# Hybrid S5 / mLSTM encoder layer: gates on 64 rows, the input factor folded into the pole powers, Toeplitz blocks copied from SBUF to SBUF, and a new planned order

## The chip, the cores and the metric

One core of one Trainium2 chip runs the whole layer in one launch. The metric is device microseconds (us) for one execution. Engines are named as the profile names them: PE (TensorE matmul, PEld its weight loads), DVE (VectorE), ACT (ScalarE), POOL (GpSimd) and SP (SyncE), whose queue issues every DMA of this kernel.

## What is computed

The reference, cut to what matters here (x is 1024 x 1024 float32; h = rmsnorm(x)):

```python
proj = h @ w_in                       # 1024 x (512 S5 | 512 x_m | 512 o | 16 gates)
# S5 group: 32 groups of 16 channels, 64 complex poles each, two directions
f = (exp(lam dt) - 1) / lam           # the input factor
s = scan(exp(lam dt), f * (B u))      # forward and reverse
y = Re(C s_f) + Re(C s_b) + d u ; y = gelu(y) ; y = y * sigmoid(y @ w_glu + b_glu)
# mLSTM group: 4 heads, two directions, chunks of 128 steps
lf = log_sigmoid(f_pre) ; b = cumsum(lf within a chunk)
m_t = max(b + m_state, max over s <= t of (b_t - b_s + li_s))   # the running maximum
m_new = max(b_last + m_state, ...) ; weights exp(d - m_t), exp(a - m_t), exp(g - m_new)
x = x + rmsnorm(concat(y_s5, y_ml) @ w_out)
x = x + rmsnorm((silu(h @ w_gate) * (h @ w_up)) @ w_down)
```

## The kernel before, in words

The kernel is recorded first and issued afterwards. Class `K` calls an engine's operation, `Rec.add` records it with a due time (`Rec.at`, from the table `PLAN`, L48), and `Rec.schedule` (L284) places all operations one after another with a cost for each (`Rec.cost`, L229; `Rec.transfer`, L267, for a DMA) under limits on SBUF pages and PSUM banks. Out comes one fixed order for each engine; `Rec.emit` (L424) issues it, so nearly every row of the profile has the line L454. Each engine works through its order strictly: a waiting instruction holds all that stands behind it, DMA issues on SP included.

The stages, in order of time:

- `w_in_a` and `w_in_tile` (L581, L660): the input projection in three products of split fp32r operands, with x and the weights loaded beside it. `evac` (L631) scales the result; the gate columns go to two 64-row tiles of which 4 rows in 32 are live.
- `s5_prelude` (L779): poles, powers 0 to 8 of each pole (`GG`), input factor `F1`, `F2`, and two tables `C1`, `C2` of 128 x 1024, which are C times the input factor (L933 to L939); a table of cosines and sines goes to DRAM (`csd`).
- `gates` (L688): log-sigmoid, cumulative sums, running maxima, four kinds of exponentials, on tiles of 64 rows by 1024 steps, eight live rows; then 16 transposes on PE and 16 small copies on ACT into `col`, and rows written to DRAM (`rowd`, `decd`) for the heads.
- `s5_main` (L980): 16 blocks. Block b makes `o1` from `G1 C1 + G2 C2`, multiplies it by B on PE, and evacuates a 16 x 2 x 240 tile `sp`. From `sp` a Toeplitz block `T` of 128 x 128 for each of two groups is made by a DMA to DRAM (`std`, L1024) and two DMAs back with overlapping rows (L1028). `T` is the weight of the first of the six output matmuls (L1055).
- `mlstm_head` (L1063): four heads, interleaved with the blocks of `s5_main`; then `glu_out`, `out_proj`, `ffn_up` and `ffn_down` (seven passes).

```python
nc.sync.dma_start(out=std[g0:g0 + 2].rearrange("g c n -> c g n"), in_=sp)          # L1024
T = self.t([128, 2, 128])
for g in range(2):
    a = std[g0 + g, :, 0:128]
    nc.sync.dma_start(out=T[:, g], in_=view(a, 0, [[16, 8], [1, 128]]))            # L1028
nc.tensor.matmul(o, lhsT=T[:, g], rhs=u[:, g], start=True, stop=False)             # L1055
```

Of the kernel before, what the change touches and what calls it, by code (L numbers as in the profile page):

```python
# [16 lines left out]
L = 1024  # L17
# [16 lines left out]
CV = dict(gpre=0, hnorm=8, skip=12, convw=16, convb=36, bglu=40, gfpre=44, gbias=52)  # L34
NCV = 53
# [124 lines left out]
class Rec:  # L160
# [68 lines left out]
    def cost(self, o):  # L229
# [3 lines left out]
        if o.fn == "dma_start":  # L233
            o.dur = 0.05
# [31 lines left out]
    @staticmethod  # L266
    def transfer(src, dst):  # L267

        def run(ap):
            r = 1  # L270
            for s, c in reversed([list(x) for x in ap]):
                if c > 1 and s != r:
                    break
                r *= c
            return r
        outer = [next((c for s, c in ap if c > 1), 1) for ap in (src, dst)]
        k = max(i for i in range(1, 17) if not outer[0] % i and not outer[1] % i)
        n = 1
        for s, c in dst:
            n *= c  # L280
        r = min(run(src), run(list(dst)[1:]) if len(list(dst)) > 1 else run(dst), 1024)
        return k, n / r / k * (0.008 + 4 * r * 0.0369e-3)

    def schedule(self):  # L284
# [32 lines left out]
        while len(order) < len(self.ops):  # L317
# [139 lines left out]
class K:  # L457
# [73 lines left out]
    def body(self):  # L531
# [22 lines left out]
        self.decd = self.d([2, 4, 8])  # L554
# [76 lines left out]
    def evac(self, kind, i, P):  # L631
# [7 lines left out]
        elif kind == "g":  # L639
            self.gi, self.gf = self.t([64, L]), self.t([64, L])  # L640
# [47 lines left out]
    def gates(self):  # L688
        nc, cv = self.nc, self.cv
        gi, gf = self.gi, self.gf  # L690
        self.col = self.t([128, 8, 2, 4, 4])
        self.dcol = self.t([128, 2, 4, 8])
        bi = cv[0:64, CV["gbias"]:CV["gbias"] + 1]
        bf = self.t([64, 1])
        nc.vector.tensor_copy(out=bf, in_=cv[64:128, CV["gbias"]:CV["gbias"] + 1])
        QA, QB = self.t([128, L]), self.t([128, L])
        a = QA[0:64]
        nc.vector.tensor_scalar(gf, gf, bf, None, ALU.add)
        nc.scalar.activation(a, gf, AF.Abs)
        nc.scalar.activation(a, a, AF.Exp, scale=-1.0)  # L700
        nc.scalar.activation(a, a, AF.Ln, bias=1.0)
        nc.vector.scalar_tensor_tensor(gf, gf, 0.0, a, ALU.min, ALU.subtract)
        mask = QB[0:64]
        nc.gpsimd.memset(mask, 1.0)
        nc.gpsimd.memset(mask[0:32].rearrange("p (c t) -> p c t", t=128)[:, :, 0:1], 0.0)
        nc.gpsimd.memset(mask[32:64].rearrange("p (c t) -> p c t", t=128)[:, :, 127:128], 0.0)
        b = gf
        f, r = slice(0, 32), slice(32, 64)
        nc.vector.tensor_tensor_scan(b[f], mask[f], gf[f], 0.0, ALU.mult, ALU.add)
        nc.vector.tensor_tensor_scan(b[r, ::-1], mask[r, ::-1], gf[r, ::-1], 0.0, ALU.mult, ALU.add)  # L710
        ev = QA[0:64]
        nc.vector.scalar_tensor_tensor(ev, gi, bi, b, ALU.add, ALU.subtract)
        z = mask
        nc.gpsimd.memset(z, 0.0)
        c3 = lambda ap: ap.rearrange("p (c t) -> p c t", t=128)
        nc.vector.tensor_copy(out=c3(z[f])[:, 1:8, 0:1], in_=c3(b[f])[:, 0:7, 127:128])
        nc.vector.tensor_copy(out=c3(z[r])[:, 0:7, 127:128], in_=c3(b[r])[:, 1:8, 0:1])
        M = gi
        nc.vector.tensor_tensor_scan(M[f], z[f], ev[f], 0.0, ALU.add, ALU.max)
        nc.vector.tensor_tensor_scan(M[r, ::-1], z[r, ::-1], ev[r, ::-1], 0.0, ALU.add, ALU.max)  # L720
        mp = self.t([64, 8, 1])
        ml = self.t([64, 8, 1])
        dc = self.t([64, 8, 1])
        nc.vector.memset(mp, 0.0)
        nc.vector.tensor_tensor(mp[f, 1:8], c3(M[f])[:, 0:7, 127:128], c3(b[f])[:, 0:7, 127:128], ALU.add)
        nc.vector.tensor_tensor(mp[r, 0:7], c3(M[r])[:, 1:8, 0:1], c3(b[r])[:, 1:8, 0:1], ALU.add)
        nc.vector.tensor_copy(out=ml[f], in_=c3(M[f])[:, :, 127:128])
        nc.vector.tensor_copy(out=ml[r], in_=c3(M[r])[:, :, 0:1])
        nc.vector.tensor_tensor(dc, mp, ml, ALU.subtract)
        nc.scalar.activation(dc, dc, AF.Exp)  # L730
        nc.vector.tensor_tensor(c3(QA[64:128]), mp.to_broadcast([64, 8, 128]), c3(M), ALU.subtract)
        nc.scalar.activation(QA[64:128], QA[64:128], AF.Exp)
        nc.vector.tensor_tensor(c3(QB[0:64]), c3(ev), ml.to_broadcast([64, 8, 128]), ALU.subtract)
        nc.scalar.activation(QB[0:64], QB[0:64], AF.Exp)
        nc.vector.tensor_tensor(QB[64:128], b, M, ALU.add)
        nc.scalar.activation(QB[64:128], QB[64:128], AF.Exp, scale=-1.0)
        for d in range(2):
            nc.sync.dma_start(out=self.rowd[0, d], in_=M[32 * d:32 * d + 4])
            nc.sync.dma_start(out=self.rowd[1, d], in_=QA[64 + 32 * d:64 + 32 * d + 4])
            nc.sync.dma_start(out=self.decd[d], in_=dc[32 * d:32 * d + 4].rearrange("p c o -> p (c o)"))  # L740
        nc.sync.dma_start(out=self.dcol.rearrange("p d h c -> p (d h c)"), in_=self.decd.rearrange("d h c -> (d h c)").partition_broadcast(128))
        for qi, Q in enumerate((QA, QB)):
            for c4 in range(2):
                P = self.psum()
                for c in range(4):
                    cc = 4 * c4 + c
                    nc.tensor.transpose(P[:, c * 128:(c + 1) * 128], Q[:, cc * 128:(cc + 1) * 128], self.ident)
                for c in range(4):
                    cc = 4 * c4 + c
                    src = P[:, c * 128:(c + 1) * 128].rearrange("p (q d x) -> p q d x", q=2, d=2)[:, :, :, 0:4]  # L750
                    nc.scalar.copy(out=self.col[:, cc, :, :, 2 * qi:2 * qi + 2].rearrange("p d h q -> p q d h"), in_=src)
# [27 lines left out]
    def s5_prelude(self):  # L779
# [60 lines left out]
        GG = [(self.t([64, 8, 2, 64]), self.t([64, 2, 64])) for _ in range(2)]  # L840
        for (g, g8), t in zip(GG, (CS, SN)):
            V.tensor_tensor(g[:, :, 0], MG[:, 0:8], t[:, 0:8], ALU.mult)
            V.tensor_tensor(g8, MG[:, 8:9].to_broadcast([64, 2, 64]), t[:, 8:9].to_broadcast([64, 2, 64]), ALU.mult)
        GR = self.t([64, 8, 2, 64])
        for r in range(2):
            nc.scalar.copy(out=GR[:, :, r], in_=GG[r][0][:, :, 0])
        for x in (0, 1):
            nc.sync.dma_start(out=self.Gd[:, :, x, :], in_=GR[x::4].rearrange("p j r s -> p j (r s)"))
        GB = self.t([64, 8, 2, 64])
        for r in range(2):  # L850
            nc.scalar.copy(out=GB[:, :, r], in_=GG[r][0][:, 7::-1, 0])
        for x in (2, 3):
            nc.sync.dma_start(out=self.Gd[:, :, x, :], in_=GB[x::4].rearrange("p j r s -> p j (r s)"))
        for g, g8 in GG:
            nc.scalar.copy(out=g[:, :, 1], in_=g[:, :, 0])
# [22 lines left out]
        F1 = self.t([64, 2, 64])  # L878
        F2 = self.t([64, 2, 64])
# [3 lines left out]
        V.tensor_tensor(F1[:, 0], a, den, ALU.mult)  # L883
# [661 lines left out]
```

## Time and profile before

| what | value |
|---|---|
| median of three runs | 1159.42 us (1158.59 to 1164.47) |
| profiled execution: its own time | 1158.98 us |
| profiled execution: span of its instructions | 1157.2 us |
| busy, share of the span | PE 94%, PEld 75%, DVE 78%, ACT 48%, POOL 1% |
| granted TensorE clock, mean | 0.971 |

The profiled execution's own time is 1.8 us more than its span, and 0.4 us under the median. Busy shares are means over stages with different limits: the table of windows in the section of rows cuts the span by stage, and the chain of waits tells what ended last in one. An instruction's duration overlaps the next one's start by some hundredths of a us, so that a sum of durations is a little more than the time taken.

### The profile page before, as it was taken

Reading aid. Unit: us, or ns where it says so; the run is one execution under the profiler, and the core shown is the slowest. Engines: PE = TensorE matmul, PEld = TensorE weight load, DVE = VectorE, ACT = ScalarE, POOL = GpSimd, SP = SyncE. Lnnn points to the kernel's source line nnn. Section 1 sums busy time; section 2 is a strip of 40 time slices with the busy share of each in tenths; the row PEclk is TensorE's granted clock in tenths of the full one; section 3 lists DMA queues with packets and bytes.
Section 4 is the critical chain, followed back from the end, with each engine's and each line's share of the span. In section 5 each row is a group of like instructions: output and inputs, shape, how many; then the busy total and the mean of one; then the engine's idle time right before and its main releaser. Section 6 shows DMA issues by size and latency. Waiting matters only on the chain.

```text
span 1157.2 us, 14999 instructions
## 1 busy us (share of the span) xinstructions
PE 1082.9 (94%) x5037; PEld 872.1 (75%) x5037; DVE 897.1 (78%) x1943; ACT 554.6 (48%) x1158; POOL 13.0 (1%) x29
## 2 busy tenths in 40 slices
PE   8988798966879999988999999999999999999997
PEld 6767686755768778767888888778787888888885
DVE  7999789889999876877857575666666589866764
ACT  6637343755759765584223232323232249443631
POOL 0000000010000000000000000000000000000000
PEclk9989899978889999999999999999999999999999
DMA  8317845774137213344332323323241488566633
GB/s 328 132 56 237 221 126 134 196 194 124 39 93 303 73 55 121 132 146 183 119 121 98 109 83 108 111 82 110 82 137 56 168 313 309 171 214 203 214 118 145
DMA packets 102109, 172.59 MB, mean 149 GB/s; under 512 B 10417, under 2 KB 39665, under 8 KB 102033
## 3 DMA queue, kind: packets, MB, share of 16 engines
q1 hardware_dynamic: 102032, 171.65, 45.2%
q8 instruction: 39, 0.64, 0.2%
q14 instruction: 38, 0.30, 0.1%
HBM read 129.63 MB, written 41.98 MB: 148 GB/s over the span
## 4 chain that ended last, share of the span: by engine, by line
PE 60%; DVE 17%; DMA 11%; ACT 7%; issue 2%; SPq 2%; DVEq 0%; ACTq 0%
PE P L454 60%; DVE s L454 17%; ACT s L454 7%; DMA s<-d 3%; DMA d<-s 3%; SPq L454 2%; DMA s<-in_w_gate 2%; DMA s<-in_xT 2%; DMA s<-in_wB 1%; DMA s<-in_B 1%; ACT L454 0%; DMA s<-in_w_up 0%; DVEq L1541 0%; ACTq L454 0%; DVEq L454 0%
## 5 line engine op out<-in xcount | busy, mean ns | idle before, releaser
L454 PE MATMUL P<-s,s 128*128 128x512 f32 (+4 forms) x4862 | 1066.5, 376 | 60.9 <-DVE s L454 27.4
L454 PEld LDWEIGHTS P<-s,s 128*128 128x128 f32 (+1 forms) x4862 | 839.3, 188 | 264.0 <-DVE s L454 35.0
L454 DVE TENSOR_TENSOR s<-s,s 128x512 fp32r<-128x512 f32 (+9 forms) x879 | 543.1, 660 | 131.4 <-ACT s L454 120.9
L454 ACT CAST s<-s 128x512 fp32r<-128x512 f32 (+4 forms) x439 | 237.6, 582 | 199.2 <-DVE s L454 71.1
L454 DVE TENSOR_TENSOR s<-P,s 128x512 f32<-128x512 f32 (+2 forms) x210 | 128.3, 622 | 84.1 <-PE P L454 55.2
L454 ACT ACTIVATE s<-s 128x1024 f32<-128x1024 f32 (+7 forms) x134 | 91.2, 689 | 186.4 <-DVE s L454 185.4
L454 ACT COPY s<-P 128x512 f32<-128x512 f32 (+6 forms) x143 | 58.9, 447 | 148.8 <-PE P L454 143.4
L454 DVE TENSOR_TENSOR s<-s 128x8 f32<-128x8 f32 (+6 forms) x194 | 66.2, 349 | 12.3 <-DMA s<-in_w_down 6.6
L454 PE MATMUL P<-s 128*128 128x512 f32 (+2 forms) x175 | 63.8, 394 | 6.2 <-DVE s L454 6.2
L454 ACT ACTIVATE s<-s,s 128x128 f32<-128x128 f32 (+3 forms) x118 | 57.3, 551 | 21.8 <-DVE s L454 9.9
L454 ACT ACTIVATE s<-P,s 128x128 f32<-128x128 f32 (+1 forms) x168 | 51.3, 390 | 9.8 <-PE P L454 8.7
L454 ACT ACTIVATE s<-P 128x512 f32<-128x512 f32 (+2 forms) x70 | 39.6, 570 | 29.8 <-PE P L454 29.2
L454 DVE SCALAR_TENSOR_TENSOR s<-s,s,s 128x1024 f32<-128x1024 f32 (+4 forms) x42 | 42.9, 1047 | 1.1 <-ACT s L454 0.9
L454 PEld LDWEIGHTS P<-s 128*128 128x128 f32 (+1 forms) x175 | 33.1, 206 | 13.4 <-DVE s L454 6.6
L454 DVE TENSOR_TENSOR_SCAN s<-s,s 128x128 f32<-128x128 f32 (+1 forms) x68 | 33.5, 518 | 0.0
L454 DVE TENSOR_SCALAR s<-s 128x1 f32<-128x1 f32 (+13 forms) x140 | 24.4, 189 | 9.8 <-ACT s L454 8.9
L454 DVE SCALAR_TENSOR_TENSOR s<-P,s,s 128x128 f32<-128x128 f32 (+1 forms) x56 | 26.7, 515 | 3.6 <-PE P L454 2.6
L454 DVE SCALAR_TENSOR_TENSOR s<-s,s 128x1024 fp32r<-128x1024 f32 (+5 forms) x30 | 23.0, 786 | 0.0
L454 ACT ACT_TABLE_LOAD x14 | 18.0, 1283 | 1.0 <-PEq L1535 0.8
L454 DVE TENSOR_TENSOR s<-s,P 128x512 f32<-128x512 f32 (+2 forms) x43 | 15.9, 377 | 1.3 <-PE P L454 1.2
L454 ACT COPY s<-s 64x512 f32<-64x512 f32 (+1 forms) x24 | 13.7, 589 | 0.3
L454 POOL TENSOR_SCALAR_AFFINE_SELECT s<-s 128x1024 f32<-128x1024 f32 (+1 forms) x9 | 10.0, 1109 | 272.0 <-DMA s<-in_wqkv 159.2
(19 smaller groups left out, 74.2 us busy)
## 6 DMA issues: line engine op xcount, KB each, us to landing
s<-d SPq DMA_DIRECT2D x125, 256.0 KB
d<-s SPq DMA_DIRECT2D x77, 256.0 KB
s<-in_w_down SPq DMA_DIRECT2D x77, 256.0 KB
s<-d SPq DMA_DIRECT2D x36, 512.0 KB
d<-s SPq DMA_DIRECT2D x28, 512.0 KB
s<-in_w_gate SPq DMA_DIRECT2D x44, 256.0 KB
s<-in_w_up SPq DMA_DIRECT2D x44, 256.0 KB
s<-in_x SPq DMA_DIRECT2D x16, 512.0 KB
```

The costliest lines, as they stand in the source:

```text
L454: getattr(getattr(nc, o.eng), o.fn)(*[g(x) for x in o.a], **{n: g(x) for n, x in o.k.items()})
```

## The change

Four edits, and a new table for the planner. `ffn_up`, `ffn_down` and `out_proj` are not edited.

1. **Gates on 64 rows.** The 16 gate rows are evacuated by two instructions into a 16 x 1024 tile and written to DRAM (`gated`); they come back as two tiles of 64 rows (direction, head, chunk) by 128 steps. Sums and maxima are taken within a row. The carry from chunk to chunk goes to DRAM (`carryd`), back as 4 rows of 8 chunks for each direction, through a scan of 7 elements, to DRAM and back as one value a row. Two transposes and one copy fill `col`.
2. **Input factor in the pole powers.** The factor multiplies the powers (64 x 9 x 64, before the transposes) instead of C. `C1` and `C2` are now loaded as they are, 128 x 1024 each, twice the bytes of `CA` and `CB` before.
3. **Toeplitz blocks SBUF to SBUF.** `std` is gone; the two DMAs of a block read `sp` itself.
4. **The planner.** An issue of a DMA costs SP 0.6 in its model (0.05 before, with a queue of 0.5 behind it); bytes are dearer; the due times and limits in `PLAN` are others.

```diff
-    win=37.832, near=7.61, res=4, tie=0.042, tensor=0.771, vector=0.602, scalar=0.107, gpsimd=0.264, sync=3.052,
-    old=14.133, pre=0.431, pre_s=0.206, gate=19.374, w=35.224, w_r=10.241, wo=109.077, wo_r=14.436, conv=75.464,
+    win=37.832, near=6.997, res=3, tie=0.042, tensor=0.771, vector=0.707, scalar=0.119, gpsimd=0.425, sync=4.338,
+    old=14.133, pre=0.234, pre_s=0.216, gate=47.675, w=35.224, w_r=9.539, wo=90.593, wo_r=19.245, conv=49.493,
...
-            o.dur = 0.05
+            o.dur = 0.6
-        return k, n / r / k * (0.008 + 4 * r * 0.0369e-3)
+        return k, n / r / k * (0.008 + 4 * r * 0.042e-3)
...
-                nc.vector.tensor_tensor(self.gi[:, c], P[hf][0:64], R[0:64, c], ALU.mult)
-                nc.vector.tensor_tensor(self.gf[:, c], P[hf][64:128], R[64:128, c], ALU.mult)
+                nc.vector.tensor_tensor(gt[:, c], P[hf][0:16], R[0:16, c], ALU.mult)
+        if kind == "g":
+            nc.sync.dma_start(out=self.gated, in_=gt)
...
     def gates(self):
-        nc.vector.tensor_scalar(gf, gf, bf, None, ALU.add)
-        nc.scalar.activation(a, gf, AF.Abs)
-        nc.vector.tensor_tensor_scan(b[f], mask[f], gf[f], 0.0, ALU.mult, ALU.add)
-        nc.vector.tensor_tensor_scan(M[f], z[f], ev[f], 0.0, ALU.add, ALU.max)
-        nc.vector.tensor_tensor(c3(QA[64:128]), mp.to_broadcast([64, 8, 128]), c3(M), ALU.subtract)
-        for qi, Q in enumerate((QA, QB)):
-            for c4 in range(2):
-                    nc.tensor.transpose(P[:, c * 128:(c + 1) * 128], Q[:, cc * 128:(cc + 1) * 128], self.ident)
+        gi, gf = self.load(rows(self.gated[0:8]), [64, 128]), self.load(rows(self.gated[8:16]), [64, 128])
+        V.tensor_tensor_scan(b[f], one[f], gf[f], 0.0, ALU.mult, ALU.add)
+        V.tensor_tensor_scan(S[f], one[f], ev[f], -3.0e38, ALU.mult, ALU.max)
+        nc.sync.dma_start(out=self.carryd[0], in_=two)
+            nc.sync.dma_start(out=X[32 * d:32 * d + 4], in_=self.carryd[0, 32 * d:32 * d + 32].rearrange("(h c) x -> h c x", c=8))
+        V.tensor_tensor_scan(mp8[0:4, 1:8], X[0:4, 0:7, 0], X[0:4, 0:7, 1], 0.0, ALU.add, ALU.max)
+            nc.sync.dma_start(out=self.carryd[1, 32 * d:32 * d + 32, 0].rearrange("(h c) -> h c", c=8), in_=mp8[32 * d:32 * d + 4])
+        nc.sync.dma_start(out=mp, in_=self.carryd[1, :, 0:1])
+        V.tensor_scalar(M, S, mp, None, ALU.max)
+        nc.tensor.transpose(P[:, 0:64], ev, self.ident[0:64, 0:64])
+        nc.tensor.transpose(P[:, 64:192], Q, self.ident)
...
+        for i, (p, q, op) in enumerate(((fr, fi, ALU.add), (fi, fr, ALU.subtract))):
+            V.tensor_tensor(F, GG[0], bc9(p), ALU.mult)
+            V.tensor_tensor(T, GG[1], bc9(q), ALU.mult)
+            V.tensor_tensor(H1[0][:, :, i], F[:, 0:8], T[:, 0:8], op)
+            V.tensor_tensor(H1[1][:, i], F[:, 8], T[:, 8], op)
...
-        for d in range(2):
-            V.tensor_tensor(c1[:, :, d], ca, f1b, ALU.mult)
-            V.tensor_tensor(tt, cb, f2b, ALU.mult)
-            V.tensor_tensor(c1[:, :, d], c1[:, :, d], tt, ALU.add)
-            V.tensor_tensor(c2[:, :, d], ca, f2b, ALU.mult)
-            V.tensor_tensor(tt, cb, f1b, ALU.mult)
-            V.tensor_tensor(c2[:, :, d], c2[:, :, d], tt, ALU.subtract)
+        nc.sync.dma_start(out=self.C1, in_=I["CA"])
+        nc.sync.dma_start(out=self.C2, in_=I["CB"])
...
-            nc.sync.dma_start(out=std[g0:g0 + 2].rearrange("g c n -> c g n"), in_=sp)
             T = self.t([128, 2, 128])
             for g in range(2):
-                a = std[g0 + g, :, 0:128]
-                nc.sync.dma_start(out=T[:, g], in_=view(a, 0, [[16, 8], [1, 128]]))
+                nc.sync.dma_start(out=T[:, g], in_=view(sp[:, g, 0:128], 0, [[16, 8], [1, 128]]))
```

**Where the order moves.** On DVE, the middle of `gates` before (s_1_145 and s_2_600 are the two gate tiles, s_1_91 the mask, P_70 and P_63 the PSUM of `evac`):

```order
L454 SCALAR_TENSOR_TENSOR s_2_600<-s_2_600,s_1_364 64x1024
L454 TENSOR_TENSOR s_1_118<-P_70,s_1_286 128x64x8
L454 SCALAR_TENSOR_TENSOR s_2_600<-s_1_91,s_2_600 32x1024 x2
L454 TENSOR_TENSOR s_1_118<-P_63,s_1_286 128x64x8
L454 SCALAR_TENSOR_TENSOR s_1_364<-s_1_145,s_1_83,s_2_600 64x1024
L454 COPY s_1_91<-s_2_600 32x7 x2
```

and now (s_1_84 holds the small tiles; s_2_678 and s_1_325 are angles of `s5_prelude`):

```order
L453 SCALAR_TENSOR_TENSOR s_2_521<-s_1_84 64x128
L453 COPY s_1_84<-s_1_84 32x1
L453 TENSOR_SCALAR s_1_118<-s_2_678 128x8x32
L453 SCALAR_TENSOR_TENSOR s_2_521<-s_1_84,s_2_521 32x128 x2
L453 TENSOR_TENSOR s_1_84<-s_1_84,s_2_521 32x1
L453 TENSOR_TENSOR s_2_678<-s_2_678,s_1_118 128x8x32
L453 TENSOR_TENSOR s_1_84<-s_1_84,s_2_521 32x1
```

The scans are an eighth as long and stand among the angles of `s5_prelude`; 20 more DVE instructions of that kind stand between the last of these rows and the scan of 7 elements that needs the carry back from DRAM.

On SP, the writes of `gates` before (d_76 is `rowd`, d_77 `decd`, d_75 `ud`, in_wB the weights of `w_in_tile`):

```order
L454 DMA d_75<-s_1_118 128x1024
L454 DMA d_76<-s_1_145 4x1024 x2
L454 DMA d_77<-s_1_83 4x8 x2
L454 DMA d_76<-s_1_364 4x1024 x2
L454 DMA d_75<-s_1_120 128x1024
L454 DMA s_1_83<-d_77 128x64
L454 DMA s_1_218<-in_wB 128x512
```

and the carry of `gates` now (d_79 is `carryd`, d_81 `csd`):

```order
L453 DMA d_79<-s_1_84 64x2
L453 DMA d_81<-s_1_90 128x4x256
L453 DMA s_1_84<-d_79 4x16 x2
L453 DMA d_81<-s_1_251 128x4x256
L453 DMA d_81<-s_1_325 128x4x256
L453 DMA d_75<-s_3_684 128x1024
L453 DMA s_1_118<-in_wB 128x512 x2
L453 DMA d_79<-s_1_84 32x1x1 x2
L453 DMA s_1_233<-d_81 64x2x512 x2
```

The carry's write, its two loads and its second write now stand in one queue with the cosine tables that the first S5 blocks load; the weights of tile 3 of the input projection, which stood right behind the gates before, are ahead of them now.

On SP, a Toeplitz block before (d_80 is `std`):

```order
L454 DMA d_80<-s_2_1183 16x2x240
L454 DMA s_1_118<-d_75 128x2x128
L454 DMA s_1_118<-d_80 128x1x128 x2
L454 DMA d_80<-s_2_1146 16x2x240
L454 DMA d_74<-s_2_1183 8x16x128 x2
L454 DMA s_2_393<-d_80 128x1x128 x2
```

and now (d_74 is `yd`, d_80 now the pole powers `Gd`):

```order
L453 DMA s_1_90<-s_1_173 128x1x128 x2
L453 DMA s_3_1063<-in_wB 128x512
L453 DMA s_1_90<-d_75 128x2x128
L453 DMA s_3_749<-in_wB 128x512
L453 DMA s_1_243<-d_80 128x1x512
L453 DMA s_1_148<-in_B 128x1x384
L453 DMA s_1_233<-s_3_749 128x1x128 x2
```

The write is gone, and with it SP's wait for its landing.

## Rows read from the trace of the kernel before

**Rows 1.** Table of windows: us, PE, PEld, DVE, ACT, POOL busy, clock, DMA share, GB/s.

```profile
44.00:345.00 301.00, 251.09 (x1349) 202.82 (x1348) 280.27 (x645) 158.90 (x344) 8.65 (x13) 0.91 0.50 136
345.00:400.00 55.00, 53.64 (x321) 45.53 (x321) 51.19 (x187) 46.45 (x102) 2.18 (x2) 0.99 0.58 210
400.00:527.00 127.00, 119.55 (x541) 94.43 (x539) 97.44 (x268) 84.37 (x243) 0.00 (x0) 1.00 0.35 118
527.00:1150.00 623.00, 621.10 (x2663) 500.13 (x2662) 428.24 (x710) 230.55 (x408) 0.00 (x0) 1.00 0.42 147
```

**Rows 2.** Chain of waits in 44 to 345 us: shares of that stretch.

```profile
by line: DVE s L454 36.7%; PE P L454 26.3%; DMA s<-d 8.6%; DMA d<-s 7.1%; ACT s L454 6.2%; SPq L454 6.0%; issue 4.6%; DMA s<-in_wB 2.2%; DMA s<-in_B 2.2%; ACT L454 0.4%; DVEq L454 0.0%; ACTq L454 0.0%
```

**Rows 3.** Chain of waits at three Toeplitz blocks: start us, us, what.

```profile
120.54 9.69 DMA s<-d
...
130.94 5.59 DMA d<-s
...
136.59 2.14 DMA s<-d
...
232.83 3.82 DMA d<-s
236.66 2.11 DMA s<-d
...
245.45 7.81 DMA d<-s
253.33 1.92 DMA s<-d
```

**Rows 4.** Waits in 44 to 345 us: total us, times, longest.

```profile
PE P L454 <- DMA s<-d: 17.1, 6, 6.1
```

**Rows 5.** Timeline: start us, us, engine, instruction, count [idle before <- releaser].

```profile
81.75 4.96 PE L454 MATMUL P<-s,s 128*128 128x128 f32 x19 [3.63 <-ACT s L454]
90.46 2.07 PE L454 MATMUL P<-s,s 128*128 128x512 f32 x4 [3.76 <-ACT s L454]
138.86 1.30 PE L454 MATMUL P<-s,s 128*128 128x128 f32 x4 [5.81 <-DMA s<-d]
140.80 0.18 DVE L454 TENSOR_TENSOR s<-P,s 16x32 f32<-16x32 f32 x1 [2.96 <-ACT s L454]
225.38 0.18 DVE L454 TENSOR_TENSOR s<-P,s 16x32 f32<-16x32 f32 x1 [3.35 <-ACT s L454]
242.13 0.18 DVE L454 TENSOR_TENSOR s<-P,s 16x32 f32<-16x32 f32 x1 [1.63 <-ACT s L454]
259.72 0.18 DVE L454 TENSOR_TENSOR s<-P,s 16x32 f32<-16x32 f32 x1 [1.55 <-ACT s L454]
```

**Rows 6.** Groups by form, DVE, 40 to 100 us: count | busy us, mean ns | idle before.

```profile
L454 DVE TENSOR_TENSOR s<-s,s 128x512 f32<-128x512 f32 x20 | 12.9, 680 | 0.0
...
L454 DVE TENSOR_TENSOR_SCAN s<-s,s 32x1024 f32<-32x1024 f32 x4 | 9.1, 2272 | 0.0
...
L454 DVE TENSOR_TENSOR s<-s,s 64x1024 f32<-64x1024 f32 x3 | 3.7, 1219 | 0.1
L454 DVE TENSOR_TENSOR s<-P,s 64x512 f32<-64x512 f32 x4 | 2.7, 686 | 0.1
...
L454 DVE SCALAR_TENSOR_TENSOR s<-s,s,s 64x1024 f32<-64x1024 f32 x1 | 1.2, 1250 | 0.0
...
L454 DVE TENSOR_SCALAR s<-s,s 64x1024 f32<-64x1024 f32 x1 | 0.7, 709 | 0.0
```

**Rows 7.** Groups by form, DVE, whole span: forms nearest to the new instructions.

```profile
L454 DVE TENSOR_TENSOR_SCAN s<-s,s 128x128 f32<-128x128 f32 x64 | 24.4, 408 | 0.0
...
L454 DVE TENSOR_TENSOR s<-s,s 64x576 f32<-64x576 f32 x4 | 3.0, 741 | 0.0
...
L454 DVE TENSOR_SCALAR s<-s 64x128 f32<-64x128 f32 x4 | 0.9, 216 | 0.0
...
L454 DVE TENSOR_TENSOR s<-s,s 64x128 f32<-64x128 f32 x3 | 0.8, 280 | 0.6 <-ACT s L454 0.5
```

More of the change, by code (lines that the diff above doesn't have):

```diff
@@ L553, in body @@
         self.rowd = self.d([2, 2, 4, L])
-        self.decd = self.d([2, 4, 8])
+        self.decd = self.d([64, 1])
+        self.gated = self.d([16, L])
+        self.carryd = self.d([2, 64, 2])
         self.xm, self.xc, self.to, self.yml = [None] * 4, [None] * 4, [None] * 4, [None] * 4
@@ L710, in gates @@
[L710 to L718, printed above, removed]
@@ L742, in gates @@
-        for qi, Q in enumerate((QA, QB)):
-            for c4 in range(2):
-                P = self.psum()
-                for c in range(4):
-                    cc = 4 * c4 + c
-                    nc.tensor.transpose(P[:, c * 128:(c + 1) * 128], Q[:, cc * 128:(cc + 1) * 128], self.ident)
[L748 to L751, printed above, removed]
+        V, A = nc.vector, nc.scalar
@@ new lines, in gates @@
+        A.activation(a, a, AF.Exp, scale=-1.0)
+        A.activation(a, a, AF.Ln, bias=1.0)
+        V.tensor_scalar(gf, gf, bf, 0.0, ALU.add, ALU.min)
+        V.tensor_tensor(gf, gf, a, ALU.subtract)
+        one = self.ones
+        V.tensor_tensor_scan(b[f], one[f], gf[f], 0.0, ALU.mult, ALU.add)
+        V.tensor_tensor_scan(b[r, ::-1], one[r], gf[r, ::-1], 0.0, ALU.mult, ALU.add)
+        V.scalar_tensor_tensor(ev, gi, bi, b, ALU.add, ALU.subtract)
+        V.tensor_tensor_scan(S[f], one[f], ev[f], -3.0e38, ALU.mult, ALU.max)
@@ new lines, in gates @@
+        V.tensor_scalar(M, S, mp, None, ALU.max)
+        for h, e in ((f, 127), (r, 0)):
+            V.tensor_scalar(ml[h], M[h, e:e + 1], -1.0, None, ALU.mult)
+        A.activation(dc, mp, AF.Exp, bias=ml)
+        A.activation(wi, M, AF.Exp, scale=-1.0, bias=mp)
+        A.activation(Q[0:64], ev, AF.Exp, bias=ml)
+        V.tensor_tensor(b, b, M, ALU.add)
+        A.activation(Q[64:128], b, AF.Exp, scale=-1.0)
+        rowd = [self.rowd[i].rearrange("d h (c t) -> (d h c) t", t=128) for i in range(2)]
@@ L839, in s5_prelude @@
         V.tensor_tensor(MG[:, 5:8], MG[:, 1:4], MG[:, 4:5].to_broadcast([64, 3, 64]), ALU.mult)
[L840 to L855, printed above, removed]
+        GG = [t9("gr"), t9("gi")]
+        for g, t in zip(GG, (CS, SN)):
+            V.tensor_tensor(g, MG, t, ALU.mult)
+        for xs, e in (((0, 1), slice(0, 8)), ((2, 3), slice(7, None, -1))):
+            GR = self.t([64, 8, 2, 64])
+            for r in range(2):
+                nc.scalar.copy(out=GR[:, :, r], in_=GG[r][:, e])
+            for x in xs:
+                nc.sync.dma_start(out=self.Gd[:, :, x, :], in_=GR[x::4].rearrange("p j r s -> p j (r s)"))
         f1_, x2, sn, cs = F[:, 1], t64("x2"), t64("sn"), t64("cs")
```

126 lines of the change are left out of this document (47 added, 79 removed).

## The prediction

> **What bounds the kernel now.** I read the table of windows first, because the page's busy shares mix stages with different limits. From 345 us on PE is the bound: busy 53.64 of 55.00 us, 119.55 of 127.00 and 621.10 of 623.00 [rows 1]. None of the edits removes work from those stages, so I carry them over as they are: 813 us that only move earlier or later as a block. The stage from 44 to 345 us is different: DVE is busy 280.27 of 301.00 us and PE 251.09, which leaves PE 50 us idle and DVE 21 [rows 1]. All four edits act there, or in the first 44 us. The chain of waits in that stage comes next: DVE has 36.7% of it, PE 26.3%, the two directions of DMA through DRAM 8.6% and 7.1%, SP's queue 6.0% [rows 2]. So no single engine makes the whole chain, but one that is busy 93% of a stage is its floor: whatever else is shortened returns at most the 21 us that DVE stands idle, while a us taken off DVE is worth up to a us.
>
> The waits show what the idle time is. PE stood 17.1 us in 6 waits for DMAs from DRAM [rows 4]. The chain shows three of those as the two legs of a Toeplitz block: 5.59 us to write and 2.14 to read back, 3.82 and 2.11, 7.81 and 1.92 [rows 3]. The timeline shows what follows from one: PE idle 5.81 us, then its matmuls, then ACT's copy of them, and a DVE instruction that stood 2.96 us for that copy; three more of that DVE form stood 3.35, 1.63 and 1.55 us [rows 5].
>
> **The change part by part.**
>
> *Gates, DVE.* Removed: four scans, 9.1 us; three 64x1024 products, 3.7; two three-operand instructions at 1.25 (I use the one row for both), 2.5; one scalar instruction, 0.7; two of the four evacuations at 0.686, 1.4 [rows 6]; some ten instructions on 1 to 8 columns, at or under the 0.18 of the 16x32 row [rows 5], 1.3. Together 18.7. Added: four scans of 128 at 0.408, 1.6; two scalar instructions at 0.216 and two products at 0.280 [rows 7], and a three-operand one priced like the products, 1.3; nine small ones, 1.3. Together 4.2. Net -14.5 us.
>
> *Gates, other engines.* PE loses 14 transposes and ACT most of the exponentials. I cost both at nothing: ACT is busy 158.90 of 301.00 us, PE idle 50 [rows 1]. PE's two waits for ACT at the gates, 3.63 us before the transposes and 3.76 before tile 3 of the input projection, whose weights stood behind the gates' writes on SP [rows 5], belong to that idle time. If the cover went, PE would lose no more than it does now.
>
> *Input factor.* Removed: twelve 128x512 products at 0.680 [rows 6], 8.2; two small powers and two copies, 0.9. Added: four 64x576 products at 0.741, two of about 512 columns at the 0.680, two of 64 columns near 0.21, and the two products of `GG` grow by 0.06 each: 4.9 [rows 6, 7]. Net -4.2. The loads of `C1` and `C2` add 0.5 MB; at the 136 GB/s of this stage that is 4 us of DMA at a mean share of 0.50 [rows 1], far ahead of the first block that reads them: nothing.
>
> *Both together* are -18.7 by durations. Those overlap a little from one instruction to the next, so I take **-18**.
>
> *Toeplitz blocks.* Sixteen writes leave SP and six DMAs of the gates come, ten issues fewer. A copy from SBUF to SBUF is not in this trace. Its near row is the read leg, with the same bytes to the same place, 1.92 to 2.14 us; the far one is the 9.69 us that another read of DRAM took on the chain [rows 3]. I take 2.1, because only the source differs. Then the write legs go: 5.59, 3.82 and 7.81 us against the PE waits there, of which the longest is 6.1 [rows 3, 4]. DVE's four waits behind them sum to 9.49 [rows 5], so the gain is 0 to 9.5. I take **-5**, about half, since the copy still has to be issued and the next thing in line (u, cosines, a free PSUM bank) is then late. At the far end each of 6 waits would grow by 9.69 less 7.73, or 12 us on PE; by DVE's part, 9.5 of 17.1, that costs +7.
>
> *The carry.* The gates now go through DRAM and back at three places where a later step waits: `gated`, and `carryd` twice; `decd` did so before too. DVE waits twice within the gates proper. Between the last sum and the scan of 7 elements its order holds 20 instructions, by the forms of rows 6 and 7 some 8 us; a round trip is 5.93 to 9.73 us by the Toeplitz legs [rows 3], plus two issues. So DVE may stand 0 to 3 us there; I take **+1.5**. The second carry has over 20 longer instructions ahead of its reader: nothing. Before these, DVE is covered by the first block's products, which the new order puts ahead of the gates.
>
> The Trainium skill, "DMA: Bandwidth & Descriptors", section "Latency and other measured facts", gives about 2 us as the fixed cost of a DMA. By that a round trip would be 4 us, this term 0 and the forecast 1.5 us lower. The rows show up to 9.73, so the sum stands on the rows.
>
> *Order.* SP's table of costs changes no work. The new order starts the S5 blocks' loads earlier and brings weights ahead of the gates' waits; it can also place a wait badly. I take 0, with 8 us either way: about as much as the whole idle time behind Toeplitz blocks.
>
> **Sum.** -18 - 5 + 1.5 + 0 = -21.5 us from the profiled execution's own 1158.98 us: **1137.5 us**. Its time is 0.4 us under the median, which I leave out. PE can take this up: it would still be idle 28 of the stage's 280 us.
>
> **The rivals.** A measurement of this kernel tells about 0.5% (6 us) from no change.
>
> *A: the gates hold SP, slower.* SP issues in order. Each of four round trips (`gated`, two of `carryd`, `decd`) has a load that cannot be issued until a write has landed; behind it stand the cosine tables and the loads of the first blocks. Priced with the longest write leg, 7.81 us, four are 31 us in which SP stands [rows 3]. It decides once that passes the work DVE has in hand: then DVE starves for the rest. All of it uncovered is 1158.98 - 21.5 + 31 = **1168 us**. For it: SP and DMA are already on the chain for a quarter of the stage [rows 2]. Against: `decd` stood like this before, and half-finished S5 products fill DVE's order there.
>
> *B: the removed work was partly cover, small gain.* Only 36.7% of the chain is DVE's [rows 2]. If what was removed beside PE's and DMA's links returns nothing, the gates' and prelude's 18 us count by about half, Toeplitz blocks and carry cancel: **1149 us**, up to 1153.
>
> *C: more than the sum.* The Toeplitz waits return all of PE's 17.1 us in place of 5, because PE then feeds DVE earlier everywhere: -18 - 17.1 + 1.5, so **1125 us**. The granted clock was 0.91 in this stage, against 1.00 in those after 400 us [rows 1]. The Trainium skill, "TensorE: Matmul & The Clock Gate", Part 1, says that the array gets 2.4 GHz after it has been busy and 1.2 after it stood idle; by that rule fewer waits also shorten matmuls, which pulls towards C. The trace agrees in so far as the stage with 50 us of idle PE is the one with the lower clock.
>
> *D: nothing moves.* The SBUF to SBUF copy is as slow as its far end (+7), the order loses 8, and half of DVE's 18 returns: -9 + 7 + 1.5 + 8 is about +7, so with any part missing the time stays **within 6 us of 1159**.
>
> **How the numbers follow.** The forecast's band, 1129 to 1145 (the order's 8 us either way), gets 0.57; B 0.17; C 0.12; D 0.07; A 0.07. The likeliest gives 1137.5. The range from 1123 to 1151 holds the band, nearly all of C and most of B. Faster by over 0.5%: 0.57 + 0.17 + 0.12 = 0.86; the same: 0.07; slower: 0.07.
>
> **What would show it.** Right: DVE's busy time falls by 16 to 19 us in all, and the stage of mixed work ends near 323 us instead of 345, with the PE-bound stages as long as before. DVE's scans of 32x1024 are gone and four of 32x128 take about 0.4 us each. Waits of PE for Toeplitz blocks fall from 17.1 to under 5 us, and the copies land in about 2 us. DVE stands under 3 us at the scan of 7 elements. Wrong: new idle time on DVE at the gates or at the first S5 blocks with SP standing for d<-s (A); DVE's idle time in the stage growing by 8 us or more (B); copies that take over 5 us (D); or a PE-bound stage after 345 us that changes by more than 5 us, which the sum has at zero.

## The result, and the profile after

The changed kernel takes 1133.16 us (median of 4, 1129.97 to 1134.88), the kernel before 1160.65 in the same comparison (1158.59 to 1164.47): a ratio of 0.9756, 95% interval 0.972 to 0.9792. The forecast was 1137.5. The total was right within 4.3 us. Its parts were not: the experiments show that the edits and the new order, which the forecast added up, are worth little apart and 27 us together.

The page's line of busy times and the table of windows after. The four windows end at the same places of the program as those of [rows 1]: the end of S5, a stretch of 55 us, the start of the up projection, the end.

```profile
PE 1073.7 (95%) x5021; PEld 870.1 (77%) x5021; DVE 879.4 (78%) x1932; ACT 547.6 (48%) x1141; POOL 11.1 (1%) x25
```

```profile
44.00:330.00 286.00, 243.04 (x1335) 196.98 (x1336) 260.18 (x633) 154.13 (x336) 7.68 (x10) 0.92 0.53 141
330.00:385.00 55.00, 54.49 (x330) 46.82 (x330) 52.99 (x193) 49.84 (x115) 2.20 (x2) 1.00 0.55 204
385.00:509.00 124.00, 118.44 (x535) 94.64 (x535) 96.14 (x258) 80.70 (x232) 0.00 (x0) 0.99 0.36 118
509.00:1126.00 617.00, 617.00 (x2662) 499.35 (x2660) 427.51 (x710) 229.49 (x403) 0.00 (x0) 1.00 0.43 148
```

Against [rows 1] the mixed stage is 15 us shorter (286 for 301): it ends at 330 us, where the forecast had 323. DVE works 20.1 us less in it (260.18 for 280.27), of which 2.5 us only moved into the first 44 us (39.03 us busy there, 36.53 before); its idle time in the stage grew, from 20.7 to 25.8 us. The stages in which PE is the bound, which the prediction carried over unchanged, are 9 us shorter: 3 us between 385 and 509, 6 us in the up and down projections (617 for 623). The chains of waits there, before (527 to 1150 us) and then after (509 to 1126 us), say where most of the 6 us lie:

```profile
by line: PE P L454 93.1%; DMA s<-in_w_gate 3.1%; DVE s L454 2.6%; ACT s L454 0.8%; SPq L454 0.3%; issue 0.2%; ACTq L454 0.0%
...
by line: PE P L453 100.1%
```

Before, the chain leaves PE at four places, where the next weights were loaded and converted late: the matmuls at 729.71, 769.40, 828.92 and 887.75 start 0.62 to 0.80 us after the one ahead, where 0.23 us is usual, 1.9 us in all. The first seven intervals of that stage, from 528.2, are 0.40 to 0.59 us, 1.5 us more; the granted clock was 0.57 there (527 to 531 us), mostly the lower of its two levels (1.2 and 2.4 GHz), after PE had idled 2.9 of the 7.6 us ahead of 527.6. The change has neither. The other 2 us or so are spread over the stage, and their cause stays open.

The chain of waits in 44 to 330 us (shares by line, as in [rows 2]), and pieces of it around the gates and the first S5 block, the last of them at a later block (start us, us, what):

```profile
by line: PE P L453 33.2%; DVE s L453 30.6%; ACT s L453 9.7%; DMA s<-d 6.1%; issue 5.8%; DMA s<-s 5.0%; DMA s<-in_wB 4.5%; DMA d<-s 2.4%; SPq L453 1.6%; ACT L453 0.9%; DVEq L453 0.1%; ACTq L453 0.0%
...
80.43 7.01 DMA s<-d
87.46 6.24 DMA s<-d
...
96.05 6.95 DMA d<-s
104.70 7.86 DMA s<-in_wB
112.63 6.37 DMA s<-s
119.14 54.84 PE P L453 x278
...
217.16 7.97 DMA s<-s
```

DVE has 30.6% where it had 36.7%, and the legs through DRAM fell from 8.6% and 7.1% to 6.1% and 2.4%. Copies from SBUF to SBUF now have 5.0%, and the two that lie on the chain take 6.37 and 7.97 us, not 2.1. The piece at 96.05 is the write of the decays (`decd`, 64 numbers). The timeline says what it costs (start us, us, engine, instruction, count, idle before and its releaser; SPq is SP's queue):

```profile
93.72 0.28 DVE L453 TENSOR_SCALAR s<-s 64x128 f32<-64x128 f32 x1 [0.63 <-DMA s<-d]
...
95.49 1.11 SPq L453 DMA_DIRECT2D d<-s  x2
...
103.07 0.95 SPq L453 DMA_DIRECT2D s<-d  x2
...
104.07 1.05 SPq L453 DMA_DIRECT2D s<-in_wB  x2
...
105.17 0.60 SPq L453 DMA_DIRECT2D s<-in_B  x1
...
112.63 1.44 SPq L453 DMA_DIRECT2D s<-s  x2
...
113.59 3.22 DVE L453 TENSOR_TENSOR s<-s,s 128x512 f32<-128x512 f32 x5 [5.12 <-DMA s<-in_B]
...
119.14 9.24 PE L453 MATMUL P<-s,s 128*128 128x128 f32 x37 [8.21 <-DMA s<-s]
```

SP issues that write at 96.05 and nothing more until 103.07, because the read of the decays is next on its queue and needs the write landed. Behind it stand the loads of S5 block 3, the weights of tile 6 of the input projection and the first Toeplitz copy. DVE then stands 5.12 us for block 3, and PE 8.21 us for the copy. The carry that the prediction priced at +1.5 shows 0.63 us, at the first row.

A second thing holds this queue. In the trace SP's DMAs mark their landing on eight semaphores in turn (101 and 104 to 110), and each issue waits until the DMA eight issues ahead of it has landed. So the read of the second carry, at 87.46 in the chain, waited for a load of cosines issued at 80.43, and the first Toeplitz copy, whose source was complete at 99.88, waited last for weights issued at 104.70. Counted by these marks, SP stood some 14 us in 21 such waits in the mixed stage, beside the 6.5 us for the decays.

PE's waits for Toeplitz blocks, total, times and longest, which stand against [rows 4]:

```profile
PE P L453 <- DMA s<-s: 13.5, 3, 8.2
```

The short scans cost what [rows 7] said (groups by form, DVE, 40 to 100 us), and of the form that the input factor's products have, that stretch holds 12 where it held 20 [rows 6]:

```profile
L453 DVE TENSOR_TENSOR s<-s,s 128x512 f32<-128x512 f32 x12 | 8.1, 680 | 0.0
...
L453 DVE TENSOR_TENSOR_SCAN s<-s,s 32x128 f32<-32x128 f32 x2 | 0.8, 410 | 0.0
L453 DVE TENSOR_TENSOR_SCAN s<-s 32x128 f32<-32x128 f32 x2 | 0.8, 410 | 0.0
```

### The profile page after: what moved, and what is told of

It reads as the page before. It is cut to its first block, busy times and chain, and to the rows that moved or that the text cites. A ratio compares the mean times of both kernels' runs of the same rounds, so it can differ in the third digit from the quotient of the medians.

```text
span 1133.2 us, 14945 instructions
## 1 busy us (share of the span) xinstructions
PE 1073.7 (95%) x5021; PEld 870.1 (77%) x5021; DVE 879.4 (78%) x1932; ACT 547.6 (48%) x1141; POOL 11.1 (1%) x25
## 4 chain that ended last, share of the span: by engine, by line
PE 70%; DVE 13%; DMA 7%; ACT 7%; issue 2%; SPq 1%; DVEq 0%; ACTq 0%
PE P L453 70%; DVE s L453 13%; ACT s L453 6%; DMA s<-d 2%; DMA s<-s 1%; DMA s<-in_wB 1%; DMA d<-s 1%; SPq L453 1%; DMA s<-in_w_glu 1%; DMA s<-in_w_gate 1%; ACT L453 0%; DMA s<-in_wA 0%; DVEq L1507 0%; DVEq L453 0%; ACTq L453 0%
## 5 line engine op out<-in xcount | busy, mean ns | idle before, releaser
L453 DVE TENSOR_TENSOR s<-s,s 128x512 fp32r<-128x512 f32 (+10 forms) x861 | 532.2, 660 | 126.6 <-ACT s L453 109.2
L453 ACT ACTIVATE s<-s 128x512 f32<-128x512 f32 (+7 forms) x133 | 86.3, 661 | 158.9 <-DVE s L453 152.6
L453 ACT COPY s<-P 128x512 f32<-128x512 f32 (+5 forms) x126 | 56.7, 481 | 146.0 <-PE P L453 137.4
L453 DVE TENSOR_TENSOR s<-s 128x256 f32<-128x256 f32 (+7 forms) x204 | 71.0, 354 | 8.7 <-ACT s L453 4.2
L453 ACT ACTIVATE s<-s,s 128x128 f32<-128x128 f32 (+4 forms) x121 | 58.2, 545 | 20.0 <-DVE s L453 9.6
L453 PE MATMUL P<-s 128*128 128x512 f32 (+1 forms) x175 | 63.0, 389 | 3.9 <-ACT s L453 2.8
L453 DVE SCALAR_TENSOR_TENSOR s<-s,s,s 128x1024 f32<-128x1024 f32 (+3 forms) x41 | 42.0, 1044 | 1.8 <-ACT s L453 1.6
L453 PEld LDWEIGHTS P<-s 128*128 128x128 f32 x175 | 33.0, 202 | 11.0 <-ACT s L453 3.2
L453 DVE TENSOR_SCALAR s<-s 128x1 f32<-128x1 f32 (+14 forms) x143 | 25.7, 191 | 10.2 <-ACT s L453 8.4
L453 DVE SCALAR_TENSOR_TENSOR s<-s,s 128x1024 fp32r<-128x1024 f32 (+4 forms) x29 | 21.9, 774 | 0.4 <-ACT s L453 0.4
L453 ACT COPY s<-s 64x512 f32<-64x512 f32 (+2 forms) x24 | 13.5, 573 | 2.8 <-DVE s L453 2.5
```

Source lines behind the costliest of these rows:

```text
L453: getattr(getattr(nc, o.eng), o.fn)(*[g(x) for x in o.a], **{n: g(x) for n, x in o.k.items()})
```

## The experiments

Each was timed in five rounds beside the kernel before. "S5 ends" is the end of PE's last matmul of the last S5 block in the profiled execution, found by counting PE's instructions in the program's order; "rest" is the span less that. Between two kernels only differences beyond their intervals count: 0.0025 is 2.9 us. The kernel before took 1159.4 to 1161.3 us in the sessions that these rows come from; the sizes below are differences of medians, and by the ratios they come out up to 2 us larger or smaller. The new table stands for the new numbers and costs together.

| kernel | median us | ratio (95%) | S5 ends | rest |
|---|---|---|---|---|
| before | 1160 | 1 | 345.2 | 812.0 |
| order_alone | 1158.08 | 0.9979 (0.9962 to 0.9997) | 351.7 | 804.9 |
| edits_old_order | 1156.48 | 0.9973 (0.9955 to 0.9992) | 348.4 | 809.7 |
| the change | 1133.16 | 0.9756 (0.972 to 0.9792) | 330.3 | 802.8 |
| bounce_back | 1134.0 | 0.9781 (0.9759 to 0.9804) | 327.2 | 804.4 |
| old_gates | 1137.88 | 0.981 (0.9784 to 0.9835) | 330.1 | 803.4 |
| old_factor | 1136.61 | 0.9794 (0.9764 to 0.9825) | 330.3 | 805.6 |
| factor_order | 1145.63 | 0.9878 (0.9855 to 0.9902) | 340.5 | 804.9 |
| table_gate | 1130.07 | 0.9738 (0.9713 to 0.9763) | 328.6 | 800.2 |
| late_dcol | 1124.3 | 0.9687 (0.9662 to 0.9712) | 320.2 | 803.4 |
| late_bounce | 1130.09 | 0.9733 (0.9709 to 0.9757) | 322.9 | 804.1 |
| late_old_factor | 1133.95 | 0.9761 (0.9735 to 0.9788) | 325.6 | 802.8 |
| late_table | 1126.1 | 0.97 (0.9675 to 0.9726) | 326.5 | 802.7 |
| late_old_order | 1150.99 | 0.9912 (0.9889 to 0.9935) | 342.0 | 809.9 |

**The order and the edits apart.** `order_alone` is the kernel before with the table and the costs of SP's model changed, `edits_old_order` the changed kernel with them put back.

```diff
-    win=37.832, near=7.61, res=4, tie=0.042, tensor=0.771, vector=0.602, scalar=0.107, gpsimd=0.264, sync=3.052,
+    win=37.832, near=6.997, res=3, tie=0.042, tensor=0.771, vector=0.707, scalar=0.119, gpsimd=0.425, sync=4.338,
...
-            o.dur = 0.05
+            o.dur = 0.6
...
-                h = max(t + 0.1, hw)
-                hw = h + 0.5
+                hw = t + 0.6
```

> The program before with only the new table of numbers and the new DMA costs in the planner. Theory (the order is what shortened the PE-bound stages, the edits what shortened the mixed one): the input projections and S5 still end near 345 us (within 3), out_proj and the up projection take some 8 us less after it, so about 1151 us. Rival 1 (the numbers were found for the new edits and mean nothing without them; the PE-bound stages gained from the edits): 1159, within 3. Rival 2 (the order is most of the whole gain): 1140 or less.

> All three edits with the table of numbers and DMA costs of before. Theory: the mixed stage ends near 331 us as it does now, and the PE-bound stages take 812 to 813 us as before: 1142 us. Rival (edits pay only in an order made for them: the gates' round trips then hold SP in front of the S5 loads): 1150 or more, with new DVE idle time at the gates. Rival (the order is worth nothing): 1134.

Measured: 1158.08 and 1156.48 us. Neither half does much; the two together give 27. My theory, that the edits had shortened the mixed stage and the order the rest, got only its second part; the time is that of the first rival, whose reason (the PE-bound stages gained from the edits) the last column refutes. For `edits_old_order` the rival of 1150 or more held, with new idle time of DVE at the gates. On the second part: with the new table the rest takes 800 to 806 us in all eleven kernels, with the old one 810 to 812 in all three. The end of S5 the table alone moved 6.5 us later and the edits alone 3.2, together they moved it 14.9 earlier. The windows of the mixed stage, `order_alone` and then `edits_old_order`, show where DVE's saved work went:

```profile
44.00:352.00 308.00, 252.85 (x1346) 202.92 (x1346) 279.41 (x636) 160.16 (x344) 9.77 (x11) 0.90 0.48 131
```

```profile
44.00:348.00 304.00, 251.80 (x1338) 203.35 (x1337) 265.04 (x639) 155.78 (x338) 8.45 (x8) 0.88 0.54 137
```

With the edits alone DVE is busy 265.04 of 304 us: 15.2 us of work gone against [rows 1], and 39.0 us idle where it was 20.7. By PE's account, its matmuls there take 251.80 us (1338 of them) at a granted clock of 0.88, where the change has 243.04 us (1335) at 0.92, each a mean over the two levels, and PE idles 52.2 us against 43.0: of the 18 us between the two stages about half is slower matmuls. The timeline of `edits_old_order` names some of the waits:

```profile
83.25 0.61 DVE L454 TENSOR_SCALAR s<-s 64x128 f32<-64x128 f32 x3 [7.03 <-DMA s<-d]
...
89.57 1.29 DVE L454 TENSOR_TENSOR s<-P,s 128x512 f32<-128x512 f32 x2 [5.39 <-PE P L454]
...
91.90 0.35 SPq L454 DMA_DIRECT2D s<-d  x1
92.30 1.85 SPq L454 DMA_DIRECT2D s<-in_wB  x4
...
98.09 1.63 DVE L454 TENSOR_TENSOR s<-s,s 128x512 fp32r<-128x512 f32 x3 [4.56 <-ACT s L454]
...
98.11 6.06 PE L454 MATMUL P<-s,s 128*128 128x512 f32 x17 [8.15 <-ACT s L454]
```

DVE stands 7.03 us for the second carry, on which the prediction spent "nothing" because 20 longer instructions stand ahead of its reader. In the new order 27 DVE instructions stand between the second carry's scan and that reader, in the old order two: the reader comes too soon. Then SP stands for the decays until 91.90, the weights of tiles 3 and 4 of the input projection go out behind that, and PE stands 8.15 us and DVE 4.56.

In `order_alone` one wait sticks out, DVE's for PE:

```profile
206.41 0.69 DVE L453 TENSOR_TENSOR s<-P,s 128x512 f32<-128x512 f32 x1 [11.75 <-PE P L453]
```

In the mixed stage, then, the new table places the old program's instructions worse than that program's own table does. The new numbers and the new costs of an issue were not tried apart.

**Is it the fit to this very program?** One number of the table moved by one, which reorders the instructions from the gates on:

```diff
-    old=14.133, pre=0.234, pre_s=0.216, gate=47.675, w=35.224, w_r=9.539, wo=90.593, wo_r=19.245, conv=49.493,
+    old=14.133, pre=0.234, pre_s=0.216, gate=46.675, w=35.224, w_r=9.539, wo=90.593, wo_r=19.245, conv=49.493,
```

> The changed kernel with one number of the table moved by one: the gates are due at 46.675 in place of 47.675, nothing else. The same instructions come out in another order from the gates on. Theory 1 (the order matters by where a few waits stand, and the table was found for this very program; any other order that the planner gives is some 10 to 20 us slower, so that most of what the two together gain is the fit and not one of the edits): 1143 to 1155 us, with the mixed stage ending 10 us later or more, the PE-bound stages as now. Theory 2 (the table as a whole, costs and due times, makes good orders for programs like this one, and a single number is worth little): 1131 to 1137.

Measured: 1130.07, ratio 0.9738, not told from the change's 0.9756. That is a us under the range of the second theory and far from the first: an order that differs in detail lost nothing. It is one such order; that the table makes good orders in general is not shown.

**One edit undone at a time, with the new table.** `bounce_back` puts the bounce through DRAM back, `old_gates` all of the gates, `old_factor` the products for `C1` and `C2`; `factor_order` has both the gates and the bounce of before.

```diff
+        std = self.d([32, 16, 240])
...
+            nc.sync.dma_start(out=std[g0:g0 + 2].rearrange("g c n -> c g n"), in_=sp)
             T = self.t([128, 2, 128])
             for g in range(2):
-                nc.sync.dma_start(out=T[:, g], in_=view(sp[:, g, 0:128], 0, [[16, 8], [1, 128]]))
+                a = std[g0 + g, :, 0:128]
+                nc.sync.dma_start(out=T[:, g], in_=view(a, 0, [[16, 8], [1, 128]]))
```

> The changed kernel with the Toeplitz blocks going through DRAM again (a write and a read each). Theory, by the term of the prediction: +5 us, 1138. Rival 1 (PE's waits for Toeplitz blocks still were 13.5 us with the copy, so the copy bought little beside other traffic): within 2 of 1133. Rival 2 (all of PE's waits come back): 1150.

> The changed kernel with the gates of before (8 rows of 1024 spread over 64 partitions) and all else as changed. Theory: DVE is busy 14.5 us longer, all of it on the path of the mixed stage: 1147 us. Rival (the three round trips through DRAM and SP's standing for them cost half of what the short scans save): 1140.

> The changed kernel with the input factor of before (C1 and C2 made by twelve products on DVE, no factor in the pole powers). Theory by the prediction's term: +4.2 us, 1137. Rival 1 (the new table with none of the edits took 1158 us and with all but the gates 1138, and the Toeplitz copy gave nothing, so the input factor is what the new order needs): 1148 or more. Rival 2 (nothing): 1133.

> The new input factor and the new table alone, on gates and Toeplitz blocks of before. If the input factor is what makes the new order pay: 1138 us, as with the gates of before and the copies. If it takes both, copies or gates with the factor: 1148 or more. If the gains only add (order -2, factor -4): 1154.

Measured: 1134.0, 1137.88, 1136.61 and 1145.63 us. By medians the copy is worth 0.8 us, the gates 4.7 and the factor 3.4 in the changed kernel; none of the three is beyond the intervals. For `bounce_back` that is the first rival (within 2 of 1133), for `old_factor` the theory; `old_gates` came out under both its figures, and `factor_order` between its first two. The gates were forecast at 14.5. The page of `old_gates`:

```profile
PE 1074.5 (95%) x5035; PEld 866.0 (76%) x5035; DVE 892.4 (79%) x1935; ACT 555.0 (49%) x1157; POOL 16.8 (1%) x29
```

DVE is busy 892.4 us in all with the old gates against 879.4, so 13 us of its work did go, and came back as waiting: S5 ends at 330.1 us with the old gates and at 330.3 with the new, and from 44 us to there DVE idles 12.3 us with the old and 25.8 with the new. The copy's worth depends on what else is there: with the old gates it is 7.8 us (1145.63 less 1137.88, ratios 0.9878 and 0.981, intervals apart). The rival of the factor, that the new order needs it, falls: without it the time is 1137.

**SP's stand for the decays taken away.** After the planner has made the order, the read of the decays is moved behind the first pair of Toeplitz copies. No other engine's order changes.

```diff
         self.rec.schedule()
+        od = self.rec.order
+        i = next(i for i, o in enumerate(od) if o.fn == "dma_start" and o.wr[0].b is self.dcol.b)
+        o = od.pop(i)
+        s5 = [j for j, q in enumerate(od) if q.fn == "dma_start" and q.rd[0].b.kind == "S" and q.wr[0].b.kind == "S"]
+        od.insert(s5[1] + 1, o)
```

> The changed kernel with one DMA moved on SP's queue: the read of the decays, for which SP stands 7 us, comes after the first Toeplitz copies in place of ahead of the loads of block 3; the other engines' orders are untouched. Theory (rival A of the prediction happens once, and PE's 8.2 us and DVE's 5.1 us of idle time near 110 us stand behind it): the first copies are issued 5 us earlier, PE's idle time there falls under 4 us, and the time falls by 3 to 6 us, to about 1129. Rival (the next in line, weights of the input projection and u, is as late, or the time is taken up by waits behind it): within 2 of 1133.

Measured: 1124.3 us, ratio 0.9687, intervals apart from the change's (0.9712 and 0.972): 8 us by the ratios and 9 by the medians, more than the 3 to 6 expected, and the fastest kernel of this study. Its timeline, with the rows that answer to those of the change:

```profile
96.84 0.59 SPq L453 DMA_DIRECT2D s<-d  x1
97.48 1.05 SPq L453 DMA_DIRECT2D s<-in_wB  x2
98.58 0.59 SPq L453 DMA_DIRECT2D s<-in_B  x1
...
107.77 1.39 SPq L453 DMA_DIRECT2D s<-s  x2
...
110.05 0.34 SPq L453 DMA_DIRECT2D s<-d  x1
...
113.68 8.56 PE L453 MATMUL P<-s,s 128*128 128x128 f32 x47 [0.96 <-DMA s<-s]
```

The loads of block 3 go out at 96.84 in place of 103.46, the first copy at 107.77 in place of 112.63, PE's wait for it is 0.96 us in place of 8.21, and DVE's 5.12 us for block 3 is gone. The window of the mixed stage:

```profile
44.00:320.00 276.00, 239.30 (x1336) 193.69 (x1336) 260.19 (x633) 153.96 (x336) 7.05 (x10) 0.94 0.56 146
```

DVE does the same 260.19 us of work in 276 us rather than 286. By PE's account 6.3 of these 10 us are less idle time (36.7 us for 43.0), and 3.7 are its matmuls: 1336 take 239.30 us, at a granted clock of 0.94 for 0.92, a mean over stretches at its two levels, 1.2 and 2.4 GHz. So some of the gain beyond the wait itself came with the clock. The Trainium skill, "TensorE: Matmul & The Clock Gate", Part 1, says that the array gets the higher level after it has been busy; these two rows agree, as the stage with less idle time of PE has the higher mean. SP is still held: its waits for the DMA eight issues ahead grow from 14 to some 19 us in the stage.

**The same prices again, without that stand.** The late read, put into four of the kernels above.

> The changed kernel with the late read of the decays, and the Toeplitz blocks through DRAM again. It prices the copy where SP no longer stands. Theory, by the prediction's term (5 us, range 0 to 9.5): 1129. Rival 1 (as between the two kernels with the early read, nothing): within 2 of 1124. Rival 2 (as with the old gates, 8 us): 1132.

> The changed kernel with the late read of the decays and the input factor of before. It prices the factor where DVE hardly stands idle. Theory by the prediction's term (4.2 us of DVE): 1128.5. Rival (the order that the planner gives is another one, and what it does is larger than the term): under 1125 or over 1133.

> The changed kernel with the gates due at 46.675 and the late read of the decays. If the two gains (3 and 9 us) are of different places: 1121. If they are both the same wait: 1124 to 1130. If DVE, which is then busy nearly throughout the mixed stage, is the floor: 1122 to 1126.

> The three edits with the old table, and the read of the decays moved on SP's queue behind the first block's Toeplitz copies; nothing else. With the old table SP stood 6.3 us for that read, with the weights of tiles 3 and 4 of the input projection next behind it, and PE and DVE stood 8.2 and 10 us there. Theory (what the old table did to the edits is this one wait): the weights go out 6 us earlier, 1148 us or less. Rival (the old order loses at several places, and what is behind this wait is late next): 1153 or more.

Measured against `late_dcol`: the copy is worth 5.8 us (1130.09, between the theory and the second rival; the intervals still overlap by 0.0003, so it is not quite clear of noise), the factor 9.7 (1133.95, the rival's range; intervals apart), the gates 13.6 (1137.88 of `old_gates`, in which SP makes no such stand; intervals apart). The moved gate number and the late read together give 1126.1, in the range for one and the same wait and not told from 1124.3; but the number's own 3 us was not clear of noise either, so that this settles little. With the old table the late read is worth 5.5 us (1150.99 for 1156.48, intervals apart), between theory and rival: the weights of tiles 3 and 4 went out 5.9 us earlier, but other waits stayed, above all the one for the second carry:

```profile
83.47 0.61 DVE L454 TENSOR_SCALAR s<-s 64x128 f32<-64x128 f32 x3 [7.14 <-DMA s<-d]
...
86.40 1.99 SPq L454 DMA_DIRECT2D s<-in_wB  x4
...
89.62 1.29 DVE L454 TENSOR_TENSOR s<-P,s 128x512 f32<-128x512 f32 x2 [5.22 <-PE P L454]
```

So the order, which the prediction took as 0 with 8 us either way, is worth 23 us with the edits (1156.48 to 1133.16) and 27 with the late read as well (1150.99 to 1124.3), and 2 us without the edits. Counted the other way, with the order first, the edits are worth 25 (1158.08 to 1133.16). Most of the gain belongs to the two together and to neither alone.

## Why the prediction was right in its total, and where its steps were wrong

**DVE's work, -18: the amount was right, what becomes of it was not.** The page shows 17.7 us less in all (897.1 to 879.4; 16 to 19 were named). By the pages 13.0 of it is the gates' (892.4 less 879.4) and 4.4 the factor's (884.1 us in `late_old_factor` less 879.7 in `late_dcol`). Of the gates' 14.5 us, 13.6 arrive in the time once SP doesn't stand for the decays, some 5, not clear of noise, in the changed kernel, and with the old table the three edits together return 3.7. "A us taken off DVE is worth up to a us" is borne out with the stress on "up to": where it went each time is the idle time of the windows, 20.7 us before, 25.8 after, 39.0 with the old table, 15.8 with the late read.

**The input factor, -4.2: undersized, or more than itself.** With SP free it measured 9.7. Its DVE time is 4.4 us, as forecast; the other order that the planner makes for the old products, and noise, are part of what was measured, and these weren't separated.

**The Toeplitz blocks, -5: right where nothing else stands, about 0 in the change.** 5.8 with the late read and 0.8 in the change, neither clear of noise, and 7.8 with the old gates, which is. The step that failed is "I take 2.1, because only the source differs": the copies on the chain took 6.37 and 7.97 us, issued among other transfers, and PE's waits for them sum to 13.5 us where under 5 were forecast. The term's size came from half of DVE's waits, not from that duration: that it held where its reason didn't is luck. Rival D, which a copy of over 5 us was to show, did not happen: the bounce is as slow in the same place (6.81 us of PE idle before the first block of `bounce_back`).

**The carry, +1.5, and "four round trips" in rival A: the place was wrong.** Neither carry made DVE stand in the changed kernel beyond 0.63 us. The second took 14.9 us there, from its first write at 78.84 to its landing at 93.70, longer than the 9.73 that the prediction had as the far end, and was hidden by the 27 instructions. The price came from `decd`, which the prediction set aside because it "stood like this before". It is rival A in the small: one stand of 7 us, not four, and it decided 8 to 9 us. The change was faster all the same: the stand came once, and the new order had put the first block's work and the weights of tiles 3 to 5 ahead of it. With the old table the second carry cost 7.03 us, so its "nothing" held for the new order only.

**The order, 0 with 8 either way: the largest error.** 23 us with the edits. Part of it, about 7 us, lies in stages where PE is the bound and which I carried over as a block; "what would show it wrong" named a change of over 5 us there, and it came. In the up and down projections most of it is PE's waits for weights, which the new order starts early enough: the chain there is PE to 98.5% in `order_alone` and to 94.1% in `edits_old_order`. The rest, some 18 us in the mixed stage, I put down to cover: the new order has work ready on DVE and transfers ahead on SP where the edits' round trips wait, the old one doesn't. The waits of 7.03 and 8.15 us in `edits_old_order` show it at two places, and taking SP's stand for the decays away there gave 5.5 us; the rest, half of it slower matmuls, is argued. I costed the order as a fourth item beside the edits; it was the condition under which they pay.

So the total owes much to luck. Taken edits first, an order worth 23 us stood at 0, while the edits, taken at 21.5 as if nothing would wait, return 4 without it; taken order first, the order is 2 and the edits 25, near the forecast's 0 and 21.5. What failed is the step that adds the two up, and with it the place: the mixed stage gave 15 of the 21.5 us, and the PE-bound stages, at nothing in the sum, gave 9. Rival B's thought, that removed work was partly cover, describes the edits alone better than the forecast did. Rival C's 1125 is nearly `late_dcol`, for another reason than the one it named.

## What to carry to other kernels

As these runs show it, work taken off a busy engine arrives in the time only if the order of every queue still has something in hand where the new waits fall: price an edit together with its order, and test each alone and both before crediting either. On an in-order queue look for a load that must wait for a write just issued ahead of it, and count all that stands behind it; here moving one such load twelve places was worth about as much as one of the edits. When edits interact, undoing them one by one in the finished kernel can understate them, because something else is then the wait: here 9 us in all (0.8, 4.7 and 3.4), where the three together are worth 25.

## What the runs showed that I had not expected

A write of 64 numbers, 256 bytes, held SP 6.95 us from its issue to the next one (96.05 to 103.07), and two copies of 64 KB within SBUF took 6.37 and 7.97 us on the chain, while the first carry's read of DRAM could be issued 3.7 us after its write (69.45 to 73.17). The Trainium skill, "DMA: Bandwidth & Descriptors", section "Latency and other measured facts", gives about 2 us as the fixed cost of a DMA, which the prediction set beside its carry term. The first carry's write is nearly twice that; the decays' write and the copies are three to four times it, with the S5 tables' writes and the blocks' loads issued around them. That this traffic is the cause was not isolated.

With the late read the prices nearly add up: gates, factor and copy singly give 13.6, 9.7 and 5.8 us, 29 in all, and all three together 34 (`order_alone` at 1158.08 to `late_dcol` at 1124.3). With intervals of some 3 us on each time, 29 and 34 are not told apart.
